# Recurrence of an RWKV-7 mixer: each head on its own rows and columns of TensorE, its two maps on top of each other

## The chip, the cores and the metric

The kernel runs on one core of a Trainium2 chip. The metric is the device time of one execution in microseconds. The kernel before took 2601.89 us (median of three runs, 2594.81 to 2606.95).

## The reference, cut to what matters

The program is one decoder block: a norm, one input projection, two causal token mixers side by side (an S5 state-space mixer and an RWKV-7 mixer), an output projection, and an MLP. The change lies in the recurrence of the RWKV-7 mixer, with 8 heads of 64 and 2048 tokens:

```python
def step(state, inp):
    r_t, d_t, k_t, v_t, kk_t, a_t = inp
    sa = jnp.einsum('bhvk,bhk->bhv', state, -kk_t)
    state = (state * d_t[:, :, None, :]
             + sa[..., None] * (kk_t * a_t)[:, :, None, :]
             + v_t[..., None] * k_t[:, :, None, :])
    return state, jnp.einsum('bhvk,bhk->bhv', state, r_t)
```

For each head a 64 by 64 state is multiplied by a decay, gets a rank-one correction from its own product with kk, and a rank-one update with v and k; the output is the state times r. All of it is float32.

## The kernel before, in words

**What runs when.** `hybrid_block` first does the S5 part and the input projection of the RWKV part (`rwkv_input`), which writes, by pair of heads, six rows of features to `f_d` in DRAM: k, v, b, a, q and bv, with the decays already worked in. `rwkv_phase` is the recurrence. Its first two blocks are prepared while `rwkv_input` still runs; the rest follows, and then the output projection and the MLP, which the change doesn't touch.

**The tiles of the recurrence.** The tokens are cut into 8 blocks of 256 (`TB`), a block into 4 chunks of 64 (`NCH`), and the 8 heads into 4 pairs (`NP`), so that a pair fills 128 partitions. One chunk is solved with matrices instead of token by token:

- `units(b, B, p)` (lines 806 to 832) takes one pair of one block. It loads b and a so that the two heads lie as blocks on the diagonal of a 128 by 128 tile (`ba`, zero elsewhere; `load_pair`, line 800, two DMAs), and a, q and k as they lie (`aq`, two DMAs). `ps_b` (line 817) multiplies b with a, q and an identity, 192 columns for each chunk; DVE masks the result and scales it into `bQ` (line 821), ACT scales the rest (line 822). `ps_a` (line 826) multiplies a with an identity and k for `aR`, 128 columns.
- `invert` (line 861) inverts 32 by 32 triangular matrices on DVE, 62 instructions a block (lines 876 and 877). Its input goes through DRAM: stores to `abd` (line 832), two loads into `M` (line 865); its result goes through `zd` (lines 880 and 882).
- `join` (line 884) couples the two halves of a chunk with matmuls of 32 by 32 (`ps_x`, line 898, first all of the one head's rows, then all of the other's; `ps_u`, line 905).
- `values(b, B, p)` (lines 834 to 859) loads k and v on the diagonal (`bk`, two DMAs), q as it lies (`qi`), and for each block q once more, transposed in its address pattern (`qS`, line 840). `ps_k` (line 853) multiplies k with q and an identity and makes `kT`; transposes (`ps_v`, line 851) make `vT`.
- `solve(B, u)` (line 908) takes one chunk: POOL builds `DT` from the inverse (four products, line 913, and two copies, line 917), `ps_pq` (line 920) multiplies it with `aR`, ACT copies the result into the diagonal blocks of `pq` in two copies (lines 923 and 924), then `ps_f` and `ps_h` (lines 928 and 930) multiply it with `bQ`. DVE adds q, the identity and `kT` (lines 934 to 936), which gives two maps: `gf` for the state and `hj` for the values.
- `chain(b, B, u, gf, hj)` (line 939) is the recurrence proper: for each pair `ps_s` accumulates `hj` with `vT` (line 949) and `gf` with the state `S` (line 951). The upper 64 rows of the result are the output, copied by ACT (line 958) and stored (line 963); the lower 64 rows times the decay (line 957, four DVE products a step, one for each half and head) are the next state, on the diagonal of `S`.

**What sets the order.** Between lines 1008 and 1073 the order of TensorE is written out by hand; the other engines are ordered by the scheduler. Step n does: the first half of the chain, the transposes left from the step before, the second half of the chain, `ps_pq` of chunk n + 2, `ps_b` of unit n + 13, `ps_k` of value n + 5, `ps_f` and `ps_h` of chunk n + 2, and `ps_a`. In the first step of a block `ps_x` and `ps_u` come in between. All loads and stores of this phase are issued by SP, in one queue, in order.

Of the kernel before, what the change touches and what calls it, by code (L numbers as in the profile page):

```python
# [15 lines left out]
P = 128  # L16
# [710 lines left out]
def consts_np():  # L727
# [10 lines left out]
    m4 = f((p // 32)[:, None] == (x // 32)[None, :])  # L738
    ist = f(s[:, None] == t64[None, :])
    parts = dict(ident=np.eye(P, dtype=np.float32), ones2=same, ma=lt, mk=ge, mb=np.concatenate([gt, ge], 1), off=off, m4=m4, ist=ist)  # L740
# [16 lines left out]
def rwkv_phase(K, f_dram, e_dram, n_dram, y_dram, ntok=2048):  # L757
# [7 lines left out]
    with ExitStack() as st:  # L765
# [6 lines left out]
        bas, aqs = [T([P, 2, NCH, P], f"ba{i}") for i in range(NB)], [T([P, 4, NCH, 64], f"aq{i}") for i in range(NB)]  # L772
        ist = c["ist"].rearrange("p (o x) -> p o x", o=1)
        for i in range(NB):
            g.memset(bas[i], 0.0)
            v.tensor_copy(aqs[i][:, 2], bc(ist, [P, NCH, 64]))
        S = None
# [3 lines left out]
        def begin(b):  # L781
# [3 lines left out]
                     abd=K.dram.tile([32, 4, 16, 32], F32, tag="abd", bufs=3, name="abd"),  # L785
# [12 lines left out]
        mask = lambda t, n: bc(t.rearrange("p (o x) -> p o x", o=1), [P, n, t.shape[1]])  # L798

        def load_pair(t, b, p, o):  # L800

            for h in range(2):
                hp = slice(h * 64, h * 64 + 64)
                nc.sync.dma_start(out=t[hp, :, :, hp].rearrange("p n c x -> p (n c) x"), in_=f_dram[p, hp, b, o:o + 2].rearrange("p n (c x) -> p (n c) x", x=64))

        def units(b, B, p):

            aR, bQ = B["aR"], B["bQ"]
            i = (b * NP + p) % NB
            ba, aq = bas[i], aqs[i]  # L810
            load_pair(ba, b, p, RW["b"])
            nc.sync.dma_start(out=aq[:, 0:2].rearrange("p n c x -> p n (c x)"), in_=f_dram[p, :, b, RW["a"]:RW["a"] + 2])
            nc.sync.dma_start(out=aq[:, 3].rearrange("p c x -> p (c x)"), in_=f_dram[p, :, b, RW["k"]])
            for uu in range(0, NCH, 2):
                psb = pp("ps_b")
                for u in range(2):
                    pe.matmul(psb[:, u * 192:(u + 1) * 192], ba[:, 0, uu + u], aq[:, 0:3, uu + u], start=True, stop=True)  # L817
# [7 lines left out]
            for u in range(NCH):  # L825
                pe.matmul(ps[:, u * P:(u + 1) * P], ba[:, 1, u], aq[:, 2:4, u], start=True, stop=True)
            v.tensor_tensor(out=aR[:, :, p, 0:64], in0=r4(ps)[:, :, 64:128], in1=mask(c["ma"], NCH), op=ALU.mult)
            act.copy(out=aR[:, :, p, 64:128], in_=r4(ps)[:, :, 0:64])
            if p == NP - 1:
                for hq in range(4):  # L830
                    q0 = (hq % 2) * 32
                    nc.sync.dma_start(out=B["abd"][:, hq], in_=bQ[hq * 32:(hq + 1) * 32, :, :, q0:q0 + 32].rearrange("s c p t -> s (c p) t"))

        def values(b, B, p):

            if p == 0:
                kv = kvs[b % 2]
                for n, shape in (("kT", [P, NCH, NP, P]), ("vT", [P, NCH, NP, P]), ("qS", [P, NP, TB])):
                    B[n] = kv.tile(shape, F32, tag=n, name=n)
                nc.sync.dma_start(out=B["qS"], in_=f_dram[:, :, b, RW["q"]].rearrange("t p n -> p t n"))  # L840
            kT, vT = B["kT"], B["vT"]
            i = (b * NP + p) % NB
            bk, qi = bks[i], qis[i]
            load_pair(bk, b, p, RW["k"])
            nc.sync.dma_start(out=qi[:, 0].rearrange("p c x -> p (c x)"), in_=f_dram[p, :, b, RW["q"]])
            for n in range(2):
                ps = pk("ps_" + "kv"[n])
                for u in range(NCH):
                    o = ps[:, u * P:(u + 1) * P]
                    if n:  # L850
                        pe.transpose(out=o, in_=bk[:, n, u], identity=K.ident)
                    else:
                        pe.matmul(o, bk[:, n, u], qi[:, :, u], start=True, stop=True)
                if n:
                    act.copy(out=vT[:, :, p], in_=r4(ps))
                else:
                    B["last"] = v.tensor_tensor(out=kT[:, :, p, 0:64], in0=r4(ps)[:, :, 0:64], in1=mask(c["mk"], NCH), op=ALU.mult)
                    act.copy(out=kT[:, :, p, 64:128], in_=r4(ps)[:, :, 64:128])
                    yield

        def invert(B, eng):

            M = un.tile([P, 32, 32], F32, tag="M", bufs=2, name="M")
            for par in range(2):
                nc.sync.dma_start(out=M[par * 64:par * 64 + 64], in_=B["abd"].rearrange("s q b t -> (q b) s t"))
# [42 lines left out]
        def solve(B, u):  # L908

            aR, kT, bQ, qS, dtc, cpl = B["aR"], B["kT"], B["bQ"], B["qS"], B["dtc"], B["cpl"]  # L910
            DT = bt.tile([P, NP, 4, 32], F32, tag="DT", name="DT")
            for p in range(NP):
                g.tensor_tensor(out=DT[:, p], in0=bc(dtc[:, u, p:p + 1, :], [P, 4, 32]),  # L913
                                in1=c["m4"].rearrange("p (a x) -> p a x", a=4), op=ALU.mult)
            for h in range(2):
                hs = slice(h * 64, h * 64 + 32)
                g.tensor_copy(DT[hs, :, 2 * h + 1], cpl[hs, u])
            ps = pb("ps_pq")
            for p in range(NP):
                pe.matmul(ps[:, p * P:(p + 1) * P], m2(DT, p), aR[:, u, p], start=True, stop=True)  # L920
            pq = pqs[u % 2]
# [66 lines left out]
        for t in pqs + Ss:  # L988
            g.memset(t, 0.0)
# [751 lines left out]
```

## Time and profile before

| what | value |
| --- | --- |
| median of three runs | 2601.89 us |
| the profiled execution's own time | 2604.97 us |
| its span, first to last instruction | 2603.2 us |
| mean granted clock of TensorE | 0.972 |
| PE busy | 2451.2 us, 94% of the span |
| recurrence after the input projection | about 655 to 991 us |
| ps_b, ps_a, ps_k, ps_pq, ps_f, ps_h | 256 instructions each |
| ps_s | 504 instructions |

A float32 matmul of the program is two pairs of a weight load (PEld) and a matmul (PE) in the trace, one pair for a transpose. In a line of a group the columns are the line, the engine, the operation, what is written and read, the shapes, the count, and then busy us, mean ns of one, and the idle time before with what ended it. For PE the two numbers such as 128*128 are rows and columns of the array that are used. Where a matmul's durations overlap, the time between the starts is its cost.

### The profile page before, as it was taken

To read this page: it belongs to the slowest core of one execution; us is meant where nothing else is said; L and a number is where in the kernel's file an instruction comes from. 1 tells how busy PE (TensorE), PEld (TensorE's weight loads), DVE (VectorE), ACT (ScalarE), POOL (GpSimd) and SP (SyncE) were. 2 spreads that over 40 slices of the span, in tenths; PEclk is the share of its full clock that TensorE was granted. 3 is DMA by queue.
4 is the path that set the end of the run, shared out by engine and by line. 5 is a ranking of instruction groups with operands and counts; after the bars stand their busy time and mean duration, and the time that the engine had idled before them with its cause. 6 is when DMAs were issued, how large, how long until landed. Compare 5 with 4: busy or idle time off the path is not lost.

```text
span 2603.2 us, 38292 instructions
## 1 busy us (share of the span) xinstructions
PE 2451.2 (94%) x13084; PEld 2030.0 (78%) x13084; DVE 1843.4 (71%) x3194; ACT 1302.0 (50%) x2551; POOL 858.4 (33%) x790
## 2 busy tenths in 40 slices
PE   7999979999898898999899999999989999999997
PEld 6887657786898887888688888888867877777775
DVE  7558797579677768666877678877766656665665
ACT  6355545465444446455476667666643323333333
POOL 1058798711222224221122320332212322332323
PEclk9999989999898998999999999999999999999998
DMA  9656737996776646443576566655495555544544
GB/s 287 206 166 177 221 115 231 251 259 176 181 153 156 145 101 199 145 149 115 178 241 216 198 208 220 242 205 198 166 355 195 175 173 164 171 158 154 186 150 166
DMA packets 540980, 491.50 MB, mean 189 GB/s; under 512 B 187281, under 2 KB 442769, under 8 KB 540785
## 3 DMA queue, kind: packets, MB, share of 16 engines
q1 hardware_dynamic: 539072, 483.54, 59.7%
q0 software_dynamic: 992, 3.67, 0.4%
q8 instruction: 104, 1.70, 0.3%
q10 hardware_dynamic: 720, 1.84, 0.2%
q14 instruction: 92, 0.75, 0.1%
HBM read 303.23 MB, written 180.49 MB: 186 GB/s over the span
## 4 chain that ended last, share of the span: by engine, by line
PE 63%; DVE 13%; DMA 10%; issue 5%; POOL 3%; ACT 3%; SPq 2%; POOLq 0%; ACTq 0%; DVEq 0%
PE ps_ua L1328 13%; PE ps_da L1328 9%; PE ps_ux L1328 7%; PE ps_dx L1328 4%; PE ps_ub L1328 3%; PE ps_db L1328 2%; DMA wraw<-in_w_down 2%; PE ps_o L435 2%; PE ps_o L433 2%; PE ps_o L434 2%; PE ps_z L433 1%; PE ps_z L434 1%; PE ps_z L435 1%; DMA hs<-hs_d 1%; PE ps_b L817 1%
## 5 line engine op out<-in xcount | busy, mean ns | idle before, releaser
L1620 POOL TENSOR_TENSOR acc<-acc,c 128x512 f32<-128x512 f32 x128 | 192.6, 1526 | 454.1 <-ACT c L1624 446.8
L1624 ACT COPY c<-ps_da 128x512 f32<-128x512 f32 x192 | 106.3, 588 | 262.6 <-PE ps_da L1328 261.1
L433 PE MATMUL ps_z<-xh,wh 128*128 128x512 f32 x448 | 183.8, 411 | 15.3 <-DVE zr L617 8.7
L435 PE MATMUL ps_z<-xh,wl 128*128 128x512 f32 x448 | 181.1, 405 | 0.0
L434 PE MATMUL ps_z<-xl,wh 128*128 128x512 f32 x448 | 180.3, 402 | 0.0
L1620 DVE TENSOR_TENSOR acc<-acc,ps_dx 128x512 f32<-128x512 f32 x128 | 87.5, 685 | 122.9 <-PE ps_dx L1328 120.7
L1425 DVE TENSOR_TENSOR wl<-wraw,wh 128x512 fp32r<-128x512 f32 x124 | 104.4, 843 | 28.1 <-ACT wh L1424 27.8
L374 ACT CAST hh<-hr 128x512 fp32r<-128x512 f32 x96 | 59.4, 620 | 117.7 <-PE ps_da L1328 90.4
L433 PEld LDWEIGHTS ps_z<-xh,wh 128*128 128x128 f32 x448 | 87.0, 194 | 40.0 <-DVE zr L617 10.5
L609 DVE TENSOR_TENSOR wl<-wr,wh 128x1024 fp32r<-128x1024 f32 x56 | 85.3, 1523 | 37.5 <-ACT wh L608 37.1
L913 POOL TENSOR_TENSOR DT<-dtc,cst 128x128 f32<-128x128 f32 x128 | 55.8, 467 | 158.2 <-PE ps_pq L920 105.9
L1291 POOL TENSOR_TENSOR ws<-wraw 128x512 f32<-128x512 f32 x28 | 41.2, 1471 | 200.6 <-DMA hs_d<-hh 72.6
L433 PE MATMUL ps_o<-woh,ys 128*128 128x512 f32 x256 | 103.0, 403 | 3.4 <-DVE xrow L1225 2.5
L1424 ACT CAST wh<-wraw 128x512 fp32r<-128x512 f32 x124 | 76.2, 617 | 52.9 <-PE ps_ua L1328 34.2
L434 PE MATMUL ps_o<-wol,ys 128*128 128x512 f32 x256 | 102.1, 399 | 0.0
L435 PEld LDWEIGHTS ps_z<-xh,wl 128*128 128x128 f32 x448 | 86.8, 194 | 19.1 <-issue 0.2
L434 PEld LDWEIGHTS ps_z<-xl,wh 128*128 128x128 f32 x448 | 87.0, 194 | 18.6 <-issue 0.9
L435 PE MATMUL ps_o<-woh,ys 128*128 128x512 f32 x256 | 100.7, 396 | 0.0
L1300 POOL TENSOR_TENSOR ws<-wraw,ws 128x512 f32<-128x512 f32 x28 | 41.7, 1489 | 176.0 <-DVE wl L1425 172.6
L1474 DVE TENSOR_TENSOR hh<-hs,hh 128x512 fp32r<-128x512 f32 x96 | 79.6, 829 | 14.2 <-ACT hh L1473 13.2
L1473 ACT CAST hh<-hs 128x512 fp32r<-128x512 f32 x96 | 59.7, 622 | 57.8 <-DVE hs L1490 21.3
L1425 DVE TENSOR_TENSOR wl<-ws,wh 128x512 fp32r<-128x512 f32 x93 | 66.7, 720 | 30.1 <-ACT wh L1424 25.9
(693 smaller groups left out, 8229.2 us busy)
## 6 DMA issues: line engine op xcount, KB each, us to landing
hs_d<-hh SPq DMA_DIRECT2D x256, 256.0 KB
hs<-hs_d SPq DMA_DIRECT2D x126, 512.0 KB
wraw<-in_w_up SPq DMA_DIRECT2D x62, 512.0 KB
wr<-in_w_in SPq DMA_DIRECT2D x56, 512.0 KB
hr<-hr_d SPq DMA_DIRECT2D x94, 256.0 KB
hr_d<-c SPq DMA_DIRECT2D x93, 256.0 KB
xrow<-in_x SPq DMA_DIRECT2D x32, 512.0 KB
wraw<-in_w_down SPq DMA_DIRECT2D x14, 1024.0 KB
```

Source lines behind the costliest of these rows:

```text
L374: nc.scalar.copy(out=hi, in_=raw)
L433: K.nc.tensor.matmul(out, lh, rh, start=i == 0, stop=False)
L434: K.nc.tensor.matmul(out, lh, rl, start=False, stop=False)
L435: K.nc.tensor.matmul(out, ll, rh, start=False, stop=i == n - 1)
L609: v.tensor_tensor(out=wl, in0=wr, in1=wh.bitcast(F32), op=ALU.subtract)
L1328: K.nc.tensor.matmul(ps, a[k], b[k], start=start and k + i == 0, stop=k == n - 1 and i == 2, skip_group_check=True)
L1424: act.copy(out=hi, in_=o)
L1425: v.tensor_tensor(out=lo, in0=o, in1=hi.bitcast(F32), op=ALU.subtract)
L1473: act.copy(out=hi, in_=o)
L1474: v.tensor_tensor(out=lo, in0=o, in1=hi.bitcast(F32), op=ALU.subtract)
L1620: add = lambda eng, o, s: eng.tensor_tensor(out=o, in0=o, in1=s, op=ALU.add)
L1624: act.copy(out=t, in_=ps)
```

## The change

The diagonal tiles go, and with them their zeros. Each head uses its own 64 rows and 64 columns of the array, and all operands are loaded as they lie in DRAM.

- `units` loads b, a and q in one DMA and k in another into one tile `rw`. `ps_b` and `ps_a` are two matmuls for each chunk, one for each head: rows `hs` of the operands, rows `hs` of the PSUM tile. Both heads write the same PSUM tile, on different partitions.
- `values` loads k and v in one DMA and q in another into `kv`. `ps_k` is done by head; its result goes to `KQ`, a tile with one map of 128 rows for each head: rows 0 to 63 what was `kT`, rows 64 to 127 what was added to the state map (q, copied by ACT, and an identity, written once at the start). The transposes now write 64 rows; they go to the upper half of `SV`. `qS` goes.
- `solve` makes `DT` with one POOL product (and two copies as before), `ps_pq` by head, one ACT copy into a dense `pq`. `ps_f` and `ps_h` become one product by head, with 64 rows and 128 columns of weights, so that the two maps come out on top of each other, each head in a PSUM tile of its own; DVE adds `KQ` with two products and gets `gh`.
- `chain` has one matmul for each head, with all 128 rows and 64 moving columns: the upper half of `SV` is the values, the lower half the state. One DVE product for each half (two a step) writes the next state into the lower half of the next chunk's `SV`.
- `abd` is laid out so that a load of `M` reads 4 KB in a piece where it read 128 bytes.

```diff
@@ rwkv_phase
-        bas, aqs = [T([P, 2, NCH, P], f"ba{i}") for i in range(NB)], [T([P, 4, NCH, 64], f"aq{i}") for i in range(NB)]
+        rws = [T([P, 5, NCH, 64], f"rw{i}") for i in range(NB)]
...
-                     abd=K.dram.tile([32, 4, 16, 32], F32, tag="abd", bufs=3, name="abd"),
+                     abd=K.dram.tile([4, 16, 32, 32], F32, tag="abd", bufs=3, name="abd"),
@@ units
-            load_pair(ba, b, p, RW["b"])
-            nc.sync.dma_start(out=aq[:, 0:2].rearrange("p n c x -> p n (c x)"), in_=f_dram[p, :, b, RW["a"]:RW["a"] + 2])
-            nc.sync.dma_start(out=aq[:, 3].rearrange("p c x -> p (c x)"), in_=f_dram[p, :, b, RW["k"]])
+            nc.sync.dma_start(out=rw[:, 0:3].rearrange("p n c x -> p n (c x)"), in_=f_dram[p, :, b, RW["b"]:RW["b"] + 3])
+            nc.sync.dma_start(out=rw[:, 4].rearrange("p c x -> p (c x)"), in_=f_dram[p, :, b, RW["k"]])
...
-                    pe.matmul(psb[:, u * 192:(u + 1) * 192], ba[:, 0, uu + u], aq[:, 0:3, uu + u], start=True, stop=True)
+                    for hs in heads:
+                        pe.matmul(psb[hs, u * 192:(u + 1) * 192], rw[hs, 0, uu + u], rw[hs, 1:4, uu + u], start=True, stop=True)
...
-                pe.matmul(ps[:, u * P:(u + 1) * P], ba[:, 1, u], aq[:, 2:4, u], start=True, stop=True)
+                for hs in heads:
+                    pe.matmul(ps[hs, u * P:(u + 1) * P], rw[hs, 1, u], rw[hs, 3:5, u], start=True, stop=True)
@@ values
+            nc.sync.dma_start(out=kv[:, 0:2].rearrange("p n c x -> p n (c x)"), in_=f_dram[p, :, b, RW["k"]:RW["k"] + 2])
+            nc.sync.dma_start(out=kv[:, 2].rearrange("p c x -> p (c x)"), in_=f_dram[p, :, b, RW["q"]])
+            ps = pk("ps_k")
+            for u in range(NCH):
+                for hs in heads:
+                    pe.matmul(ps[hs, u * P:(u + 1) * P], kv[hs, 0, u], kv[hs, 2:4, u], start=True, stop=True)
+            for h in range(2):
+                hp = slice(h * 64, h * 64 + 64)
+                B["last"] = v.tensor_tensor(out=KQ[0:64, :, h, p, 0:64], in0=r4(ps)[hp, :, 0:64], in1=mask(c["mk"][hp], NCH, 64), op=ALU.mult)
+                act.copy(out=KQ[0:64, :, h, p, 64:128], in_=r4(ps)[hp, :, 64:128])
+                act.copy(out=KQ[64:128, :, h, p, 0:64], in_=kv[hp, 2])
+            yield
+            ps = pk("ps_v")
+            for u in range(NCH):
+                pe.transpose(out=ps[0:64, u * P:(u + 1) * P], in_=kv[:, 1, u], identity=K.ident)
+            act.copy(out=SV[0:64, :, p], in_=r4(ps)[0:64])
@@ invert
-                nc.sync.dma_start(out=M[par * 64:par * 64 + 64], in_=B["abd"].rearrange("s q b t -> (q b) s t"))
+                nc.sync.dma_start(out=M[par * 64:par * 64 + 64], in_=B["abd"].rearrange("q b s t -> (q b) s t"))
@@ solve
-            for p in range(NP):
-                g.tensor_tensor(out=DT[:, p], in0=bc(dtc[:, u, p:p + 1, :], [P, 4, 32]),
-                                in1=c["m4"].rearrange("p (a x) -> p a x", a=4), op=ALU.mult)
+            g.tensor_tensor(out=DT, in0=bc(dtc[:, u].rearrange("p a (o t) -> p a o t", o=1), [P, NP, 2, 32]),
+                            in1=bc(c["m2"].rearrange("p (o a t) -> p o a t", o=1, a=2), [P, NP, 2, 32]), op=ALU.mult)
...
-                pe.matmul(ps[:, p * P:(p + 1) * P], m2(DT, p), aR[:, u, p], start=True, stop=True)
-            pq = pqs[u % 2]
-            psr = ps.rearrange("p (a q x) -> p a q x", a=NP, q=2)
-            act.copy(out=pq[0:64, :, :, 0:64], in_=psr[0:64])
-            act.copy(out=pq[64:128, :, :, 64:128], in_=psr[64:128])
+                for hs in heads:
+                    pe.matmul(ps[hs, p * P:(p + 1) * P], m2(DT, p)[hs], aR[hs, u, p], start=True, stop=True)
+            pq = bt.tile([P, NP, P], F32, tag="pq", name="pq")
+            act.copy(out=f2(pq), in_=ps)
             yield
-            psf, psh = pb("ps_f"), pb("ps_h")
-            for p in range(NP):
-                pe.matmul(psf[:, p * P:(p + 1) * P], pq[:, p, 1], bQ[:, u, p, 64:192], start=True, stop=True)
-            for p in range(NP):
-                pe.matmul(psh[:, p * P:(p + 1) * P], pq[:, p, 0], bQ[:, u, p, 64:192], start=True, stop=True)
...
+            ph = [pb("ps_h") for _ in range(2)]
+            for p in range(NP):
+                for h in range(2):
+                    hs = slice(h * 64, h * 64 + 64)
+                    pe.matmul(ph[h][:, p * P:(p + 1) * P], pq[hs, p], bQ[hs, u, p, 64:192], start=True, stop=True)
+            gh = bt.tile([P, 2, NP, P], F32, tag="gh", bufs=3, name="gh")
+            for h in range(2):
+                B["last"] = v.tensor_tensor(out=f2(gh[:, h]), in0=ph[h], in1=f2(B["KQ"][:, u, h]), op=ALU.add)
@@ chain
-                    pe.matmul(pss[:, o], hj[:, p], vT[:, u, p], start=True, stop=S is None)
-                    if S is not None:
-                        pe.matmul(pss[:, o], gf[:, p].rearrange("p q x -> p (q x)"), S[:, p], start=False, stop=True)
+                    for h in range(2):
+                        o = (2 * (p - p0) + h) * 64
+                        pe.matmul(pss[:, o:o + 64], gh[:, h, p], SV[:, u, p, h * 64:h * 64 + 64], start=True, stop=True)
...
-                for h in range(2):
-                    hs = slice(h * 64, h * 64 + 64)
-                    e = em[64:128, p0:p0 + 2, h, b * NCH + u:b * NCH + u + 1]
-                    v.tensor_tensor(out=new[hs, p0:p0 + 2, hs], in0=pv[64:128, :, h], in1=bc(e, [64, 2, 64]), op=ALU.mult)
+                if n + 1 < nb * NCH:
+                    to = SVs[(n + 1) // NCH % 2][64:128, (n + 1) % NCH, p0:p0 + 2].rearrange("p a (h x) -> p (a h) x", h=2)
+                    v.tensor_tensor(out=to, in0=pss[64:128, 0:2 * P].rearrange("p (a x) -> p a x", a=4),
+                                    in1=bc(em[64:128, 2 * p0:2 * p0 + 4, n:n + 1], [64, 4, 64]), op=ALU.mult)
@@ set-up
-            g.memset(bks[i], 0.0)
-            v.tensor_copy(qis[i][:, 1], bc(ist, [P, NCH, 64]))
+        for t in KQs:
+            for h in range(2):
+                for u in range(NCH):
+                    v.tensor_copy(t[64:128, u, h, :, 64:128], bc(ist[64:128], [64, NP, 64]))
+        g.memset(SVs[0][64:128, 0], 0.0)
```

More of the change, by code (lines that the diff above doesn't have):

```diff
@@ L737, in consts_np @@
     off = f((h[:, None] == (x // 64)[None, :]) & ((s < 32)[:, None]) & ((x % 64 >= 32)[None, :]))
-    m4 = f((p // 32)[:, None] == (x // 32)[None, :])
+    m2 = f((s // 32)[:, None] == (t64 // 32)[None, :])
     ist = f(s[:, None] == t64[None, :])
-    parts = dict(ident=np.eye(P, dtype=np.float32), ones2=same, ma=lt, mk=ge, mb=np.concatenate([gt, ge], 1), off=off, m4=m4, ist=ist)
+    parts = dict(ident=np.eye(P, dtype=np.float32), ones2=same, ma=lt, mk=ge, mb=np.concatenate([gt, ge], 1), off=off, m2=m2, ist=ist)
     offs, o = {}, 0
@@ L797, in rwkv_phase @@
         r4 = lambda t: t.rearrange("p (c x) -> p c x", c=NCH)
-        mask = lambda t, n: bc(t.rearrange("p (o x) -> p o x", o=1), [P, n, t.shape[1]])
-        def load_pair(t, b, p, o):
-            for h in range(2):
-                hp = slice(h * 64, h * 64 + 64)
-                nc.sync.dma_start(out=t[hp, :, :, hp].rearrange("p n c x -> p (n c) x"), in_=f_dram[p, hp, b, o:o + 2].rearrange("p n (c x) -> p (n c) x", x=64))
+        mask = lambda t, n, rows=P: bc(t.rearrange("p (o x) -> p o x", o=1), [rows, n, t.shape[1]])
+        heads = [slice(h * 64, h * 64 + 64) for h in range(2)]
         def units(b, B, p):
             aR, bQ = B["aR"], B["bQ"]
-            i = (b * NP + p) % NB
-            ba, aq = bas[i], aqs[i]
-            load_pair(ba, b, p, RW["b"])
-            nc.sync.dma_start(out=aq[:, 0:2].rearrange("p n c x -> p n (c x)"), in_=f_dram[p, :, b, RW["a"]:RW["a"] + 2])
-            nc.sync.dma_start(out=aq[:, 3].rearrange("p c x -> p (c x)"), in_=f_dram[p, :, b, RW["k"]])
+            rw = rws[(b * NP + p) % NB]
+            nc.sync.dma_start(out=rw[:, 0:3].rearrange("p n c x -> p n (c x)"), in_=f_dram[p, :, b, RW["b"]:RW["b"] + 3])
+            nc.sync.dma_start(out=rw[:, 4].rearrange("p c x -> p (c x)"), in_=f_dram[p, :, b, RW["k"]])
             for uu in range(0, NCH, 2):
@@ L831, in units @@
                     q0 = (hq % 2) * 32
-                    nc.sync.dma_start(out=B["abd"][:, hq], in_=bQ[hq * 32:(hq + 1) * 32, :, :, q0:q0 + 32].rearrange("s c p t -> s (c p) t"))
+                    nc.sync.dma_start(out=B["abd"][hq].rearrange("b s t -> s b t"), in_=bQ[hq * 32:(hq + 1) * 32, :, :, q0:q0 + 32].rearrange("s c p t -> s (c p) t"))
         def values(b, B, p):
[L836 to L859, printed above, removed]
+            KQ, SV = KQs[b % 2], SVs[b % 2]
@@ L934, in solve @@
-            v.tensor_tensor(out=gf[:, :, 0], in0=pf[:, :, 0], in1=qS[:, :, u * 64:(u + 1) * 64], op=ALU.add)
-            v.tensor_tensor(out=gf[:, :, 1], in0=pf[:, :, 1], in1=bc(ist, [P, NP, 64]), op=ALU.add)
-            B["last"] = v.tensor_tensor(out=f2(hj), in0=psh, in1=f2(kT[:, u]), op=ALU.add)
-            yield gf, hj
-        def chain(b, B, u, gf, hj):
-            nonlocal S
-            vT = B["vT"]
+                for h in range(2):
+                    hs = slice(h * 64, h * 64 + 64)
+                    pe.matmul(ph[h][:, p * P:(p + 1) * P], pq[hs, p], bQ[hs, u, p, 64:192], start=True, stop=True)
```

36 lines of the change are left out of this document (15 added, 21 removed).

## The prediction, made before the changed kernel was run

> **What bounds the kernel now.** I read the page first, then busy time by stretch over the recurrence, the timeline of TensorE inside one step, the chain of waits, the queue of SP, and last the groups of DVE and ACT there. The page:
>
> ```profile
> span 2603.2 us, 38292 instructions
> PE 2451.2 (94%) x13084; PEld 2030.0 (78%) x13084; DVE 1843.4 (71%) x3194; ACT 1302.0 (50%) x2551; POOL 858.4 (33%) x790
> ```
>
> PE carries the kernel, but an average says nothing of the stage that changes. That stage runs from about 655 to 991 us. I cut it where a block of four steps begins (a step is 64 tokens, a block 256); columns are length, then busy PE, PEld, DVE, ACT, POOL, the granted clock, and the DMA share:
>
> ```profile
> 655.60:706.30 50.70, 44.98 (x402) 42.54 (x402) 31.20 (x102) 21.53 (x55) 15.04 (x36) 0.86 0.82 181
> 706.30:744.90 38.60, 37.32 (x403) 36.34 (x402) 33.08 (x118) 18.36 (x47) 10.14 (x27) 1.00 0.71 158
> 744.90:793.50 48.60, 42.41 (x403) 41.38 (x402) 35.44 (x123) 20.63 (x51) 10.08 (x28) 0.86 0.68 154
> 793.50:837.40 43.90, 39.80 (x403) 39.06 (x403) 33.89 (x118) 19.79 (x49) 10.05 (x27) 0.92 0.68 156
> 837.40:879.10 41.70, 38.63 (x403) 37.89 (x402) 33.37 (x118) 19.61 (x48) 10.09 (x27) 0.96 0.71 162
> 879.10:915.40 36.30, 32.75 (x369) 31.91 (x368) 29.30 (x102) 16.84 (x39) 9.36 (x24) 1.00 0.54 116
> 915.40:946.70 31.30, 28.56 (x338) 27.57 (x337) 24.08 (x75) 12.92 (x27) 8.58 (x22) 1.00 0.46 109
> 946.70:991.00 44.30, 39.00 (x402) 37.04 (x403) 27.18 (x65) 24.97 (x49) 11.42 (x26) 0.96 0.55 164
> ```
>
> The four blocks in the middle do the same work (403 instructions of PE) in 38.6, 48.6, 43.9 and 41.7 us. The first is the clean one: PE at full clock, 1.3 us idle. The others lose 3 to 10 us to idleness and to the low clock behind it. DVE needs 33 to 35 us, so it is the next limit, close under PE. One step on PE:
>
> ```profile
> 810.98 0.49 PE L949 MATMUL ps_s<-vT,hj 128*128 128x128 f32 x2
> ...
> 811.97 0.60 PE L851 MATMUL ps_v<-cst,bk 128*128 128x128 f32 x4
> ...
> 813.30 1.06 PE L920 MATMUL ps_pq<-aR,DT 128*128 128x128 f32 x8
> 814.20 1.47 PE L817 MATMUL ps_b<-aq,ba 128*128 128x192 f32 x8
> 815.50 1.05 PE L853 MATMUL ps_k<-qi,bk 128*128 128x128 f32 x8
> 816.39 1.06 PE L928 MATMUL ps_f<-bQ,pq 128*128 128x128 f32 x8
> 817.28 1.06 PE L930 MATMUL ps_h<-bQ,pq 128*128 128x128 f32 x8
> 818.18 1.06 PE L826 MATMUL ps_a<-aq,ba 128*128 128x128 f32 x8
> 819.07 0.39 PE L949 MATMUL ps_s<-vT,hj 128*128 128x128 f32 x2
> ```
>
> The step takes 8.09 us with no hole. By differences of starts, a group of eight instructions takes 0.89 us at 128 columns (0.111 each; each f32 matmul of the program is two of them) and 1.30 us at 192. ps_s, in pieces from 810.98 to 813.30 less the transposes' 0.44, has 16 instructions at 0.111, 1.78 us.
>
> The lost time is seen in the chain of waits, and in SP's queue before it:
>
> ```profile
> 822.15 5.56 DMA lo<-zd
> 827.76 2.05 PE ps_k L853 x8
> 829.80 1.71 PE ps_f L928 x8
> ```
>
> ```profile
> 815.30 2.71 SPq L865 DMA_DIRECT2D M<-abd  x2
> 818.05 1.50 SPq L963 DMA_DIRECT2D y_d<-Y  x1
> 820.84 1.27 SPq L804 DMA_DIRECT2D bk<-f_d  x2
> ```
>
> PE stands still until 827.76 and then does eight instructions in 2.05 and 1.71 us instead of 0.89. The chain names lo, but ps_k reads bk, issued just ahead of lo on the same queue; bk waited behind the inverter's M loads, which SP needs 2.71 us to issue.
>
> **The change part by part.** (1) The products per head. ps_b, ps_a, ps_k and ps_pq become two matmuls of 64 rows and 64 columns each, on opposite corners of the array, with as many moving columns as before. One after the other they would cost twice; side by side, the same. Does this array run two such matmuls together? The trace has one place where neighbours use different rows: ps_x does 32 instructions on rows 0 to 31 and then 32 on rows 64 to 95. Counting what is in flight at one instant (a window of a nanosecond; PE first, PEld second):
>
> ```profile
> 837.70:837.70 0.00, 0.00 (x6) 0.00 (x4) 0.00 (x0) 1.00 0.00 0
> 838.38:838.38 0.00, 0.00 (x9) 0.00 (x6) 0.00 (x0) 1.00 1.12 256
> 838.70:838.70 0.00, 0.00 (x6) 0.00 (x3) 0.00 (x0) 1.00 0.00 0
> ```
>
> In the middle of either run six matmuls and three or four loads are in flight; where the row groups change, nine and six. So matmuls and weight loads of different row groups do overlap, in f32, some three deep, and a stream that alternates heads every two instructions asks for less than that. I take full overlap: cost 0 against before. The other end is none: 1.30 + 0.89 + 0.89 + 0.89 = 3.97 us more in each of the 32 steps.
>
> (2) The maps. ps_f and ps_h (16 instructions, 1.78 us) become 16 on halves of the rows, in pairs with a PSUM bank each: 0.89 us by the same overlap. Their weights are 64 rows of 128 columns. A load of 128 columns after another:
>
> ```profile
> 846.50 0.30 PEld L949 LDWEIGHTS ps_s<-vT,hj 128*128 128x128 f32 x2
> ```
>
> Two loads of 0.192 us end 0.30 after the first began: 0.108 apart. If loads of the two halves took turns, ps_h would stay at 16 x 0.108 = 1.73 us; the six loads in flight above speak for overlap. I take 0.89, a saving of 0.89. The Trainium skill, TensorE: Matmul & The Clock Gate, section "LDWEIGHTS (loading the stationary operand)", says a load's time goes with its columns alone, so that half the rows save nothing; 128/1.2 ns is 107 ns, which the trace's 0.108 bears out, and if such loads also took turns the saving would be 0.05.
>
> (3) The state. ps_s keeps 16 instructions with 64 columns instead of 128, but still 128 columns of weights each. At 0.108 a load they cannot come faster than 16 x 0.108 = 1.73 us: saving 0.05, at the very best 0.89.
>
> (4) Leaving and entering small tiles. ps_b straight behind ps_x's 32 by 32 tiles, and ps_b in a step without them:
>
> ```profile
> 839.47 1.50 PE ps_b L817 x8
> ...
> 849.88 1.30 PE ps_b L817 x8
> ```
>
> That is 0.20 us for one change of tile shape. A step gets up to four (full to 64x64 at ps_pq, to 64x128 at ps_h, back at ps_a, full at ps_s): 0 to 0.8 us; I take 0.4, since a change may be milder between halves. The transposes for V keep all rows and only write fewer columns: 0.
>
> PE per step: -0.89 - 0.05 + 0.4, about -0.5, 2 us a block.
>
> (5) Loads. Each units and each values pass issued two loads of 64 x 8 pieces of 256 bytes beside its plain ones; now it has two loads with rows of 1 to 3 KB, and the 512 KB for qS are gone. M was 2 x 2048 pieces of 128 bytes; now 64 rows of 4 KB, so SP's 2.71 us should fall to about twice the 0.64 that one of L804's takes (1.27 for two). So SP gives out the values' load some 3 us or more sooner, into rings that carry less. The load landed 5.6 us behind its issue; I expect the stall and the low clock behind it to go nearly entirely. What is late next is PE itself.
>
> (6) The other engines, by groups between 700 and 980 us:
>
> ```profile
> L957 DVE TENSOR_TENSOR S<-ps_s,em 64x128 f32<-64x128 f32 x116 | 34.1, 294 | 12.4 <-PE ps_s L951 10.0
> L936 DVE TENSOR_TENSOR hj<-ps_h,kT 128x512 f32<-128x512 f32 x29 | 19.9, 686 | 3.5 <-PE ps_h L930 2.3
> L924 ACT COPY pq<-ps_pq 64x512 f32<-64x512 f32 x30 | 17.4, 581 | 0.7
> L934 DVE TENSOR_TENSOR gf<-ps_f,qS 128x256 f32<-128x256 f32 x29 | 12.2, 421 | 11.0 <-PE ps_f L928 10.9
> L857 DVE TENSOR_TENSOR kT<-ps_k,cst 128x256 f32<-128x256 f32 x27 | 11.3, 418 | 9.9 <-PE ps_k L853 9.7
> ```
>
> DVE: four state products of 0.294 become two of 64x256 (priced as L934's 0.421), -0.34; L934, L935 and L936, 0.42 + 0.42 + 0.69, become two of L936's size, -0.15; the mask product L857 becomes two on 64 rows, +0.42. Nothing in sum, so DVE's 33 us a block stay and are the floor. ACT: the two pq copies (0.58 each) become one, and three short ones come (two for q into KQ, and KQ's copy out of PSUM in two halves), at most 0.58 each; with 20 busy of 40 us this hides, and the one on the way from ps_pq to ps_h is 0.58 shorter. POOL's four DT products become one and its zero fills go: hidden, off the path. At the start DVE gets 16 small identity copies for KQ, at most 0.4 each by L934: hidden in the 19.5 us that it idles from 655.6 to 706.3, and 2 us late where they are not.
>
> The sum, against the profiled 2604.97 us (span 2603.2 and 1.8 around it; the median of the runs is 3 us lower). Clean block: 37.3 - 2 of PE and 1.3 idle is 36.6; I allow 37.5. Four of them against 38.6 + 48.6 + 43.9 + 41.7 = 172.8: 150, -23. The stretches from 879.1, 915.4 and 946.7: -2 of PE each, and some 1 of idleness from the shorter copy: -9. The first, 655.6 to 706.3, at clock 0.86: -3. The eight units of the first two blocks run earlier, between full-size products, and pay two changes of shape each, 16 x 0.2 = +3; the identity copies +2. In all -30: 2575 us.
>
> **The rivals.** (A) Slower: the two heads do not run together where they write one PSUM bank. In ps_x the two runs wrote different banks; ps_b, ps_a, ps_k and ps_pq write theirs into one, on different partitions, and no row here shows that. Price: 32 x 3.97 = 127 more, ps_f's 28 less, 13 for changes of shape, and of the stalls 25 saved: 2605 + 87 = 2692. Since a full miss is 127 and the forecast 30, it decides from the point where a quarter of the pairs fail to overlap. The Trainium skill, TensorEngine Tiling (Array Packing), section "Restrictions and Gotchas", states that different row tiles cannot access the same PSUM bank simultaneously; by that rule this is the outcome, though it does not say whether column halves on separate partitions count, and no run here shows it. Chance 0.17.
>
> (B) No change: the map products do not get shorter because their loads take turns (1.73 us, as above). 32 x 0.84 = 27 of the 30 are gone: 2602. The same comes out if every change of shape costs 0.2 and part of the stalls stays. For it: DVE at 33 of 38 us leaves little slack, so each late operand shows. Against it: loads in flight six deep. Chance 0.17.
>
> (C) Faster still: ps_s goes by its 64 moving columns, 32 x 0.84 = 27 more: 2548. Against it, the 0.108 of a load; DVE's floor would catch it too. Chance 0.06.
>
> **How the numbers follow.** Forecast 0.60, of which its own bounds (changes of shape 0 to 0.8 us a step, 13 us each way; half of the 25 us of stalls) make 2555 to 2595. No change of this kernel under about 0.5% (13 us) can be told from nothing. Faster: 0.56 of the forecast and all of C, 0.62. Same: most of B and the forecast's upper edge, 0.17. Slower: A and a little of B, 0.21. For eight in ten the range reaches from 2550 to 2620; A and most of C are left out.
>
> **What would show it.** PE in a step: ps_b still 1.3 us and ps_a, ps_k, ps_pq 0.89 for twice the instructions, with starts in pairs; ps_h alone 0.89; ps_s about 1.75. Blocks of 36 to 38 us, full clock, no hole ahead of ps_k; SP issuing M in about a microsecond; the DMA share under 0.6; DVE's busy time a block unchanged. The prediction is wrong if ps_b takes 2.6 us (A), if ps_h stays at 1.7 (B), or if holes of 3 us remain ahead of ps_k.

## The result, and the profile after

The changed kernel takes 2681.62 us (median of four runs, 2677.86 to 2689.64) against 2599.59 us before: a ratio of 1.0318, 95% interval 1.0298 to 1.0337. It is slower by about 80 us; the forecast was 2575, with a range of 2550 to 2620. The page of the profile after:

```profile
span 2680.8 us, 40056 instructions
PE 2493.5 (93%) x14116; PEld 2035.4 (76%) x14116; DVE 1853.0 (69%) x3144; ACT 1320.5 (49%) x2615; POOL 818.5 (31%) x687
```

PE is busy for 42 us more than before, with nearly the same share of the span (93% for 94%). The recurrence, cut where ps_x starts, as it was cut for before (length, then busy PE, PEld, DVE, ACT, POOL, the granted clock, DMA share, GB/s):

```profile
658.40:719.70 61.30, 49.77 (x587) 42.40 (x588) 38.75 (x129) 26.87 (x72) 5.15 (x14) 0.81 0.49 136
719.70:771.80 52.10, 44.53 (x532) 38.70 (x530) 34.90 (x110) 21.79 (x57) 5.87 (x15) 0.79 0.41 110
771.80:827.60 55.80, 45.41 (x531) 39.96 (x529) 35.05 (x110) 21.80 (x57) 5.86 (x15) 0.78 0.39 103
827.60:880.10 52.50, 44.05 (x532) 38.25 (x531) 34.98 (x110) 21.86 (x57) 5.88 (x15) 0.83 0.41 109
880.10:935.50 55.40, 46.22 (x532) 40.35 (x531) 35.02 (x110) 21.86 (x57) 5.88 (x15) 0.78 0.39 103
...
1016.20:1073.00 56.80, 41.05 (x451) 37.52 (x448) 33.85 (x58) 28.54 (x56) 19.71 (x21) 0.79 0.53 167
```

The stretches come in the same order as before's, one for one. Before, the four whole blocks took 38.6 to 48.6 us; now they take 52 to 56, the stretch ahead of them 61.3 for 50.7, the one at the end 56.8 for 44.3. From the first cut to the last the recurrence takes 414.6 us, where it took 335.4, so the whole loss lies in it. DVE's busy time in a block is 35 us (33 to 35 before), and the DMA share fell from 0.7 to 0.4, both about as predicted. But PE idles 7.6 to 10.4 us in each block, and runs at a granted clock of 0.78 to 0.83 around that.

One block by its four steps says where. First the kernel after: the step ahead of ps_x, the step with ps_x, and the two that follow. Then the kernel before, whose lines begin with the step with ps_x and end with the step ahead of the next ps_x:

```profile
861.80:878.20 16.40, 10.85 (x103) 9.37 (x102) 15.09 (x53) 4.85 (x13) 0.72 (x1) 0.80 0.28 80
878.20:897.90 19.70, 16.35 (x230) 14.16 (x229) 11.17 (x34) 7.33 (x18) 1.89 (x6) 0.73 0.38 96
897.90:908.00 10.10, 9.93 (x103) 9.10 (x105) 4.54 (x12) 3.86 (x11) 1.98 (x6) 0.83 0.25 41
908.00:917.10 9.10, 7.90 (x100) 6.79 (x100) 4.13 (x12) 5.13 (x14) 1.29 (x3) 1.00 0.76 223
```

```profile
836.40:848.80 12.40, 12.40 (x198) 12.08 (x197) 11.20 (x38) 6.75 (x16) 2.96 (x8) 1.00 0.59 162
848.80:857.20 8.40, 8.40 (x72) 8.25 (x71) 8.00 (x32) 4.20 (x11) 2.40 (x6) 1.00 0.61 130
857.20:865.20 8.00, 8.00 (x71) 8.00 (x70) 4.21 (x13) 3.43 (x9) 2.98 (x9) 1.00 1.02 171
865.20:878.10 12.90, 9.83 (x71) 9.56 (x70) 9.97 (x36) 5.34 (x14) 1.75 (x4) 0.87 0.69 178
```

Read the DVE column. DVE's work in a block is the same, but in the changed kernel 15.09 us of it (53 instructions) stand in the step of 16.4 us, 11.17 in the next, and 4 us in each of the last two, where DVE has nothing to do for half of the time. Of those 53 instructions, 41 are the inverter's products (counted in the trace); the four lines hold 41, 18, 0 and 3 of them. Before, the lines quoted hold 24, 16, 2 and 19, the first 40 the end of one inverse, the other 21 the beginning of the next. From its first product to its last, an inverse in the middle blocks takes 24 us in the changed kernel and 34 to 36 in the kernel before. The step with 15 us of DVE work lasts 16.4 us, though TensorE is busy in it for 10.85. What PE waits for in it:

```profile
861.76 1.09 PE L911 MATMUL ps_pq<-aR,DT 64*64 64x128 f32 x16
862.68 1.47 PE L811 MATMUL ps_b<-rw 64*64 64x192 f32 x16
865.78 1.09 PE L840 MATMUL ps_k<-kv 64*64 64x128 f32 x16 [1.64 <-ACT SV L850]
868.30 2.08 PE L920 MATMUL ps_h<-bQ,pq 64*128 64x128 f32 x16 [1.42 <-ACT pq L913]
870.30 1.74 PE L821 MATMUL ps_a<-rw 64*64 64x128 f32 x16
...
875.57 1.06 PE L849 MATMUL ps_v<-cst,kv 128*64 128x128 f32 x4 [2.50 <-ACT KQ L844]
```

The brackets are idle time and what ended it: ACT copies, but these stand behind others for which ACT waited for DVE. The products of DVE in that time:

```profile
866.88 0.43 DVE L940 TENSOR_TENSOR SV<-ps_s,em 64x256 f32<-64x256 f32 x1
867.34 0.28 DVE L868 TENSOR_TENSOR Z<-Z,prod 128x115 f32<-128x115 f32 x1
867.65 0.28 DVE L867 TENSOR_TENSOR prod<-Z,M 128x110 f32<-128x110 f32 x1
...
869.89 0.30 DVE L868 TENSOR_TENSOR Z<-Z,prod 128x133 f32<-128x133 f32 x1
870.22 0.35 DVE L815 SCALAR_TENSOR_TENSOR bQ<-ps_b,n,cst 128x128 f32<-128x128 f32 x1
```

Between the second state product (L940) and the first scaling of ps_b's result (L815) nine of the inverter's instructions (L867, L868) take 2.9 us, in DVE's fixed order, while ps_b has been there since about 864. That state product itself comes 5 us after its ps_s, which ended at 861.8, with products of the inverter in between; ACT's copy of the output waits for it until 867.40, the copy of pq follows on ACT at 867.67, and ps_h can start at 868.30. The step with ps_x has a second queue in it, ACT's:

```profile
838.12 0.37 ACT L844 COPY KQ<-ps_k 64x256 f32<-64x256 f32 x1 [0.49 <-DVE KQ L843]
842.64 0.83 ACT L845 COPY KQ<-kv 64x256 f32<-64x256 f32 x2 [4.15 <-DMA kv<-f_d]
843.49 0.37 ACT L823 COPY aR<-ps_a 128x256 f32<-128x256 f32 x1
843.76 1.17 ACT L897 COPY cpl<-ps_u 32x512 f32<-32x512 f32 x2
```

The two new copies of q into KQ (L845) wait 4.15 us for the load of q, and the copies of ps_a's and ps_u's results, which ps_pq needs (the second by way of DT), wait behind them. Over 700 to 1050 us the view of waits has for this:

```profile
ACT KQ L845 <- DMA kv<-f_d: 44.5, 19, 5.9
```

(44.5 us in total, 19 times, the longest 5.9.) Two causes are thus in sight: the place of the inverter in DVE's order (theory 1), and the q copies in ACT's queue (theory 2). The rival, theory 3: the halved tiles, or the longer chain into KQ (DVE, ACT, DVE, ACT where it was DVE, ACT), are slow by themselves.

### The profile page after: what moved, and what is told of

Its sections match the earlier page's. It is cut to its first block, busy times and chain, and to the rows that moved or that the text cites. A ratio compares the mean times of both kernels' runs of the same rounds, so it can differ in the third digit from the quotient of the medians.

```text
span 2680.8 us, 40056 instructions
## 1 busy us (share of the span) xinstructions
PE 2493.5 (93%) x14116; PEld 2035.4 (76%) x14116; DVE 1853.0 (69%) x3144; ACT 1320.5 (49%) x2615; POOL 818.5 (31%) x687
## 4 chain that ended last, share of the span: by engine, by line
PE 49%; DVE 6%; DMA 5%; ACT 2%; issue 1%; POOL 1%; SPq 0%; POOLq 0%; ACTq 0%; DVEq 0%
PE ps_ua L1312 13%; PE ps_da L1312 9%; PE ps_ux L1312 7%; PE ps_dx L1312 4%; PE ps_ub L1312 3%; DMA wraw<-in_w_down 3%; PE ps_db L1312 2%; PE ps_o L433 2%; PE ps_o L434 2%; PE ps_o L435 2%; DMA hs<-hs_d 1%; DVE acc L1604 1%; PE ps_s L936 1%; POOL acc L1604 1%; DVE wraw L1299 1%
## 5 line engine op out<-in xcount | busy, mean ns | idle before, releaser
L1284 POOL TENSOR_TENSOR ws<-wraw,ws 128x512 f32<-128x512 f32 x28 | 41.7, 1488 | 176.8 <-DVE wl L1409 167.5
L903 POOL TENSOR_TENSOR DT<-dtc,cst 128x256 f32<-128x256 f32 x32 | 24.0, 751 | 222.4 <-PE ps_pq L911 173.9
L815 DVE SCALAR_TENSOR_TENSOR bQ<-ps_b,n,cst 128x128 f32<-128x128 f32 x128 | 43.0, 348 | 64.4 <-PE ps_b L811 32.3
```

## The experiments

**The inverse left out, in both kernels** (called a_inv0 and b_inv0; a stands for the changed kernel, b for the kernel before). 60 of the 62 products of an inverse are not done.

```diff
-            for s in range(31):
+            for s in range(1):
```

> The changed kernel with 60 of the 62 DVE products of each 32 by 32 inverse left out (so the inverse is not computed). Theory 1, order on DVE: the inverter's products stand in runs of two to nine in front of the products that PE and ACT wait for, in two of the four steps of a block. Without them these two steps (16.4 and 19.7 us) fall to the 8.5 us of the other two plus 4 for the 32 by 32 tiles: a block of 52 to 56 us falls to about 38, five blocks, 2682 - 75 = about 2605, granted clock in the blocks near 1.0. Theory 2, ACT's queue: the q copies wait for loads just as before, 2650 or more. Theory 3, the halved tiles themselves run slowly or cold: the clock in the blocks stays at 0.8 and the time above 2660.

> The kernel before with the same 60 products of each inverse left out: the control. Theory 1: its order spreads the inverter's products thinly, so they cost it little, the stalls at ps_k being of the loads: blocks of 40 to 43 instead of 43.2 us, 2580 to 2600. If DVE bounds both kernels alike, it gains as much as the changed one, some 75 us.

Measured: a_inv0 2616.83 us, 65 less than the changed kernel, ratio to before 1.0045 (1.0026 to 1.0064). b_inv0 2567.87, ratio 0.9872 (0.9846 to 0.9897): 36 less than before. A block of b_inv0, and one of a_inv0:

```profile
739.10:775.80 36.70, 36.70 (x402) 36.26 (x401) 20.09 (x57) 19.59 (x49) 9.73 (x27) 1.00 0.80 185
```

```profile
842.70:885.50 42.80, 37.70 (x531) 32.96 (x529) 19.38 (x49) 21.78 (x56) 5.09 (x12) 0.92 0.50 135
```

With the inverse gone, TensorE never idles in this block of the kernel before, at a DMA share of 0.8, and the holes ahead of ps_k are gone with it: they were not a matter of the loads alone, as the prediction had it. (The view of waits of b_inv0 has no load ahead of ps_k, and its middle blocks all take 36.7 to 36.9 us.) In a_inv0 the middle blocks take 41.7 to 47.4 us: the steps without ps_x take 7.4 to 10, but the step with ps_x still takes 18 to 22, where b_inv0 has 12.5. So theory 1's 2605 was missed by 12 us, and b_inv0 gained more than theory 1 allowed it. Without the inverse the changed kernel is still 49 us slower than the kernel before without it: the inverter is a part of the loss, and not all of it.

**q by DMA** (a_qdma): theory 2 alone.

```diff
-                act.copy(out=KQ[64:128, :, h, p, 0:64], in_=kv[hp, 2])
+                nc.sync.dma_start(out=KQ[64:128, :, h, p, 0:64], in_=f_dram[p, hp, b, RW["q"]].rearrange("p (c x) -> p c x", x=64))
```

> The changed kernel with q brought into the lower rows of KQ by two DMAs in place of ACT's two copies. Theory 2, ACT's queue: the 44 us in which ACT stands in front of these copies waiting for a load go, and what is behind them (the copies of cpl and of pq) comes earlier: about 2640. Theory 1: only the part of them that ends in PE's wait for DT in the step after ps_u goes, 2 us a block: 2665 to 2680.

**The inverter spread** (a_spread): theory 1 alone. Its pairs of products are tied singly behind other DVE products, 9, 9, 9 and 4 pairs in four steps.

```diff
+                if inv is not None:
+                    k = min(QUOTA[u], left)
...
+                    for j in range(k):
+                        with tc.issue_after(marks[j * len(marks) // k]):
+                            next(inv)
```

> The changed kernel with all its work, but the inverter's products tied one pair at a time behind the other DVE products of four steps (9, 9, 9 and 4 pairs) in place of all in two steps. Theory 1: no run of them is longer than about 1 us, blocks fall from 54 to about 40 us: 2600 to 2620. Theory 2 or 3: 2660 or more.

**Both** (a_spread_qdma).

> The changed kernel with both suspects taken away at once: the inverter's pairs of products are tied one by one behind other DVE products over four steps (9, 9, 9, 4), and q reaches KQ by two DMAs in place of two ACT copies. Theory 1 (the order of the inverter on DVE) and theory 2 (q copies that hold ACT's queue) together: each alone left the step with ps_x at 17 to 18.5 us; if nothing else delays it, it falls to about 12.5 to 13.5, as in the kernel before, the blocks are 37 to 40 us, and the time is 2656 less 4 blocks of 4 us and some for the first stretch, 2620 to 2640. If the chain KQ DVE, ACT, DVE, ACT by itself delays it (third theory), the step stays at 17 or more and the time within 10 us of 2656.

Measured: a_qdma 2676.10 us (ratio to before 1.0279, 1.0252 to 1.0306), a_spread 2655.73 (1.0206, 1.0185 to 1.0226), both 2644.13 (1.0139, 1.0116 to 1.0162). So the q copies are worth some 5 us, within what theory 1 expected and far from theory 2's 2640; the inverter spread is worth 26, which lies between what theory 1 (2600 to 2620) and the others (2660 or more) expected. Two steps of a_spread, the one ahead of ps_x and the one with it:

```profile
841.90:849.80 7.90, 7.86 (x103) 6.99 (x102) 6.89 (x25) 4.06 (x11) 0.77 (x3) 1.00 0.59 136
849.80:867.00 17.20, 14.94 (x229) 12.81 (x228) 12.62 (x38) 8.38 (x21) 1.97 (x4) 0.80 0.44 132
```

The step ahead of ps_x falls from 16.4 to 7.9 us: theory 1 is right there. The step with ps_x stays at 17 to 18.6 us in the middle blocks of all three, so the two theories, as stated, don't cover it, and 2644 lies 4 us over the range that they gave; the step is what the third theory expected, though the time is 2 us under its 10 us around 2656. But the trace of both together shows another thing. ps_x of the block from 846 us starts 2.05 us late, because DVE's transpose of the inverse waits 2.37 us for the inverse to come back by DMA. Over 700 to 1050 us the view of waits has for this:

```profile
PE ps_x L896 <- DVE up L886: 15.6, 5, 5.1
```

The changed kernel and a_qdma have no such wait, a_spread has 10.4 us of it: spreading the inverse has made it. DVE's product for aR and its state products stand behind that transpose, up to 848.6, and ACT behind them: it idles 6.1 us until 847.4, and the copies of ps_x's result come at 850.0 and 850.6, with ps_x done at 849.0. That is an order too, only not one of the two that were removed.

**The orders of DVE and ACT by hand** (a_hand; the same for the kernel before, b_hand). Both engines, like TensorE, now follow the order in which the program writes the steps, with the inverter's pairs written singly between the other products. (In the cut below, tick() writes the next pair of the inverter, if the step's share isn't used up.)

```diff
-        with tc.manual_schedule(engines={mybir.EngineType.PE}):
+        QUOTA = (9, 9, 9, 4)
+        with tc.manual_schedule(engines={mybir.EngineType.PE, mybir.EngineType.DVE, mybir.EngineType.Activation}):
...
                 B["last"] = v.tensor_tensor(out=f2(gh[:, h]), in0=ph[h], in1=f2(B["KQ"][:, u, h]), op=ALU.add)
+                tick()
...
-                        for _ in invert(Bs[m // NP], v):
-                            pass
+                        iv.update(it=invert(Bs[m // NP], v, True), left=31)
+                        next(iv["it"])
```

> The changed kernel, with the order of DVE and ACT, too, as the program writes it through the recurrence, and the inverter's pairs written singly between the products of the steps (9, 9, 9, 4 a block). If the orders on DVE and ACT alone lost the time (theories 1 and 2 as one: the arithmetic on TensorE is sound, the queues around it are not), blocks fall to 36 to 40 us, the last stretch to 41 us, and the time to 2585 to 2620. If the smaller tiles themselves or the KQ chain lose it, blocks stay at 43 or more, and the time over 2640.

> The kernel before with the same orders written out by hand and the same quotas of the inverter. It says what the order alone is worth: before's blocks of 38.6, 48.6, 43.9 and 41.7 fall to 37 to 38 us if its stalls were the inverter's place on DVE (as its run with the inverse left out had 36.8), and the time to 2570 to 2585. If the late load of bk was the cause, as the prediction had it, blocks stay above 42 and the time at 2590 or more. The change by itself is then read from the pair a_hand and b_hand.

> a_hand with the q copies of ACT replaced by two DMAs into KQ. If ACT's queue still stands behind the q load (theory 2) with its order written out, this is 5 us or more a block faster than a_hand; if the order alone was it, the two agree within 10 us.

Measured: a_hand 2610.03 us, ratio to before 1.0015 (1.0001 to 1.0029). No operation was changed or left out, and some 72 of the 80 us are back. Two blocks of a_hand, the step with ps_x, and another step on TensorE:

```profile
746.10:784.90 38.80, 36.46 (x530) 32.09 (x531) 33.22 (x110) 21.94 (x56) 5.78 (x15) 1.00 0.54 144
...
823.80:862.60 38.80, 36.45 (x529) 32.06 (x529) 33.21 (x110) 21.95 (x56) 6.07 (x16) 1.00 0.56 145
...
822.30:835.80 13.50, 12.19 (x230) 10.78 (x229) 11.85 (x36) 7.40 (x18) 1.81 (x4) 1.00 0.46 138
```

```profile
853.27 1.09 PE L930 MATMUL ps_pq<-aR,DT 64*64 64x128 f32 x16
854.19 1.47 PE L823 MATMUL ps_b<-rw 64*64 64x192 f32 x16
855.49 1.04 PE L854 MATMUL ps_k<-kv 64*64 64x128 f32 x16
856.46 1.16 PE L939 MATMUL ps_h<-bQ,pq 64*128 64x128 f32 x16
857.56 1.09 PE L834 MATMUL ps_a<-rw 64*64 64x128 f32 x16
858.58 1.10 PE L956 MATMUL ps_s<-SV,gh 128*128 128x64 f32 x8
859.67 0.63 PE L864 MATMUL ps_v<-cst,kv 128*64 128x128 f32 x4
860.13 1.00 PE L956 MATMUL ps_s<-SV,gh 128*128 128x64 f32 x8
861.06 1.09 PE L930 MATMUL ps_pq<-aR,DT 64*64 64x128 f32 x16
```

DVE does the same work, 33 us, in a block of 38.8, TensorE has the full clock in these two blocks and 0.96 in the two other middle ones, and the step with ps_x takes 13.5 to 14.6 us (12.4 before) with the chain into KQ and with the q copies as the change wrote them. Theory 3 falls but for a microsecond or two in that step, and the q copies do no harm where they stand in their turn: a_hand_qdma, at 2619.85 (1.0052, 1.0033 to 1.0072), is 10 us slower than a_hand.

b_hand did not gain: 2625.08 (1.0070, 1.0046 to 1.0094), slower than before, with blocks of 44 us, where 37 to 38 was expected if the inverter's place was what stalled the kernel before. Its ps_x waits for the inverse's way back (15.8 us over 700 to 1050 us). An order by hand is no gain as such; for that kernel the scheduler's own was better.

**Each queue alone, and a fairer partner** (a_hand_dve, a_hand_act: only the one engine's name in the set; b_hand_q: the kernel before by hand with shares 11, 11, 9, 0).

> a_hand, with only DVE's order as the program writes it (and the inverter's pairs singly between the steps' products); ACT's order is left to the planner again. If DVE's queue carries the loss, blocks stay at 38.8 to 40 us and the time within 12 us of a_hand (2600 to 2622). If ACT's queue (q copies and up copies that stand ahead of what is due) carries it, blocks go back to 45 or more, and the time to 2640 or more.

> a_hand, with only ACT's order as the program writes it; DVE's order is left to the planner. The mirror of the run with DVE's alone: if DVE's queue carries the loss, blocks stay at 48 us or more, and the time over 2650; if ACT's does, blocks fall under 42 us, and the time to 2600 to 2625. Should both runs stop half way (blocks of 43 to 45, 2630 to 2650), the loss is in the two orders together, neither queue alone.

> The kernel before with its orders written out, and the inverter's shares 11, 11, 9, 0 in place of 9, 9, 9, 4, so that the inverse is written out and read back one step earlier. In b_hand the product of up waited for that way back (17 us of waits at ps_x between 700 and 1050 us; the step ahead of ps_x took 19 us), so it was no fair partner of a_hand. If that was its loss, the step falls to 8 to 13 us, blocks to 37 to 39 us, and the time to 2575 to 2595, and what the change does to TensorE alone is then about nothing or a loss beside a_hand's 2610. If it stays at 2615 or more, the loss lies in something else of the order.

Measured: a_hand_dve 2624.45 (1.0068, 1.0042 to 1.0094), a_hand_act 2684.48 (1.0298, 1.0269 to 1.0326), b_hand_q 2622.02 (1.0064, 1.0040 to 1.0087). A middle block of a_hand_dve, and one of a_hand_act:

```profile
795.50:836.10 40.60, 37.66 (x529) 32.74 (x529) 33.55 (x109) 21.84 (x56) 5.75 (x16) 0.96 0.53 144
```

```profile
831.70:885.20 53.50, 43.38 (x532) 37.72 (x530) 34.37 (x110) 22.98 (x59) 5.84 (x15) 0.81 0.42 110
```

DVE's order carries most of the loss: mended alone it gives 57 of the 80 us (blocks of 40.6 to 41.4 us, a little over what was expected); ACT's, alone, nothing; ACT's after DVE's is mended, 14 more. One rival is left: SP's queue was not written by hand, but the scheduler gave it another order along with DVE's, so loads came at other times. The traces speak against it. In the changed kernel, over 700 to 1050 us, PE waits for no load of the recurrence; ACT's q copies wait 44.5 us for theirs, and in a_hand_dve they still wait 37.4 us, with 57 us of time gained.

In b_hand_q the wait of ps_x is mostly gone, as expected (4.5 us are left; blocks still 44 to 45), and now TensorE waits for what a load brings:

```profile
PE ps_k L867 <- DMA lo<-zd: 16.2, 4, 4.6
```

That is the hole that the prediction described, four times up to 4.6 us in this window, of 700 to 950 us; in the changed kernel with its orders by hand, same window, ps_k waits for no load. As in the prediction, the name lo is the last load of the queue and ps_k's own is another; which one held it was not tried.

**The last stretch** (a_hand_tail, a_hand_tail2, a_best). In a_hand the recurrence ended at 996 us, 9 us after before's, with work of the next phase ahead of the last steps' products. a_hand_tail ties that work on DVE and ACT behind the third step from the end; a_hand_tail2 ties it on DVE, ACT and TensorE behind the last map; a_best also moves the last inverse forward (shares 11, 16, 4, 0).

```diff
+            with tc.issue_after(K.tail[0]), tc.issue_after(K.tail[1]), tc.issue_after(K.tail[2]):
                 opened = out_proj(K, keep,
...
```

> a_hand with the work of the phase behind the recurrence (splits of its weights, its first sums) queued on DVE and ACT behind the first state of the third step from the end. In a_hand such work stands ahead of the last steps' products, with TensorE idle for 3.6, 3.5 and 6.1 us between 962 and 993 us of its span; the last state product is at 996.0 where the kernel before has it at 987.3. If that order is the whole of the lost tail, the last ps_s comes at 982 to 986 and the time falls by 5 to 12 us under a_hand, to 2598 to 2605, just under the kernel before. If the next phase lives on that early work, the end of the recurrence moves and the time does not: within 4 us of a_hand.

> a_hand with all instructions of the phase behind the recurrence queued on DVE, ACT and TensorE behind the last gh, pq and ps_h product of the recurrence. In the run that tied them on DVE and ACT alone, three steps from the end, a transpose of the next phase (ps_gt) stood ahead of ps_h on TensorE and waited for its load (3.6 us of idleness), and gh stood 8 us behind weight splits. If the mixed tail is what keeps the version with the orders by hand from beating both kernels, the last ps_s comes at 980 to 986 in place of 996 to 998, and the time at 2590 to 2600, ratio 0.995 to 0.999. If that early work is needed where it stands, the time stays within 4 us of 2607, or rises.

> The changed kernel with orders by hand and the tail tied, and the last inverse's shares 11, 16, 4, 0 in place of 9, 9, 9, 4. In the run without this the last inverse ended at 927.6 us of the span, its way out and back put the product of up at 939.2, and ps_x of the last block at 940.7, 41.1 us behind the one before it, where the kernel before has 31.3. If that lateness alone holds the last block, ps_x comes at 930 to 934, the last ps_s at 974 to 978, and the time at 2592 to 2600, ratio about 0.996: a version faster than both. If another chain holds it, or the saving is taken up by the phase behind, the ratio stays within 0.998 to 1.001.

Measured: 2606.47 us (ratio 1.0009, 0.9993 to 1.0025), 2605.73 (0.9994, 0.9981 to 1.0008) and 2602.68 (1.0001, 0.9986 to 1.0017). The first did not move the end of the recurrence (998 us), since TensorE still stood at a transpose of the next phase:

```profile
972.57 0.48 PE L1149 MATMUL ps_gt<-cst,grow 128*128 128x128 f32 x1 [3.67 <-DMA grow<-g_d]
972.98 2.08 PE L939 MATMUL ps_h<-bQ,pq 64*128 64x128 f32 x16
```

With that tied too, the last ps_s came at 983.1 us, as expected, and in a_best at 980.5, against 987.3 before. The time of the whole kernel did not follow: all three are the kernel before within 0.3%. a_best missed its ps_x (937.5 us, where 930 to 934 was expected), its last ps_s (974 to 978) and with them the 2592 to 2600 us that hung on these. No version tried that does all the work is faster than the kernel before.

## Why the prediction was wrong, point by point

- **(1) The products per head: right.** In a_hand's step the 16 instructions of ps_pq take 0.92 us, those of ps_b 1.30, of ps_k 0.97 (starts to next starts); one after the other would be 1.78 and 2.60. Rival A named this as the place where the kernel would lose, at 2692 us. The time came out near that by luck, not by its mechanism: both heads write one PSUM tile and run side by side. The Trainium skill, TensorEngine Tiling (Array Packing), section "Restrictions and Gotchas", says that different row tiles cannot access the same PSUM bank at the same time; here that doesn't hold, for these tiles lie on opposite corners and differ in columns, too. For column tiles the Trainium skill, PSUM — Partial Sum Buffer, section "PSUM bank collisions raise a hardware error", allows one bank on disjoint partitions, and the 0.92 us agrees with that.
- **(2) The maps: right in the mechanism.** ps_h takes 1.10 us with its change of shape where ps_f and ps_h took 1.78. Rival B's first way, loads that take turns, falls. Its time, 2602, is what came out with the orders by hand and the tail tied, and for it the prediction had a second way: changes of shape, and DVE with little slack.
- **(3) The state: right, and a little worse.** Each half of ps_s takes 0.93 to 1.09 us for eight instructions, 1.78 in all before and 2.02 now: half the moving columns, with weights of 128 columns still, gained nothing. Rival C falls. The Trainium skill, TensorE: Matmul & The Clock Gate, section "LDWEIGHTS (loading the stationary operand)", says that a load's time goes with its columns; the trace agrees, with 0.116 us each in the faster half where it was 0.111.
- **(4) Changes of shape: mis-sized.** A step of a_hand without a hole takes 7.79 us against 8.09 before: -0.3, where the sum had -0.5. By block, TensorE is busy 36.45 us at full clock against b_inv0's 36.70 without a hole, so the change saves TensorE about a quarter of a microsecond a block, and not 2.
- **(5) The loads: right in what the change does, wrong in what follows.** M is issued in less than before's 2.71 us, though not in the 1.27 or so that was forecast (the queue's row after, its line of SP):

```profile
852.78 1.87 SPq L856 DMA_DIRECT2D M<-abd  x2
```

  The DMA share fell to 0.4, and no load stands ahead of ps_k any more. Two steps failed here. The first is the cause of the lost time before, put down to the late load alone: b_inv0 does the same loads and has no wait of ps_k for one, with blocks of under 37 us, and the view of waits before has no more than 11.5 us of ps_k waiting for a load in the whole recurrence (660 to 990 us). The second is "What is late next is PE itself." What was late next was DVE. With it went the 23 us that four blocks were to save; they lost 43 instead (215.8 us for 172.8).
- **(6) The other engines: this failed with it.** "Nothing in sum, so DVE's 33 us a block stay and are the floor" is right as a sum and says nothing of the steps. 33 of 38 us is a floor only if the work lies evenly; with 15.1 us of it in one step of four, that step is about as long as DVE is busy. And "with 20 busy of 40 us this hides" left out that ACT works in order: a copy that waits 4 us for its load holds those behind it, though a_qdma shows that this alone costs some 5 us. All of the 0.21 for a slower kernel was given to A and a little of B; no rival had the orders of DVE and ACT in it. The prediction took the orders of DVE and ACT as they were, though the scheduler makes them anew for each kernel.
- **The clock** went with it, and more than doubled the price. In the block from 880.1 us, 9.2 us of idleness come with a granted clock of 0.78, at which the same 530 instructions keep PE busy 46.22 us; in a_hand it is 36.45 at 1.00. Of the 16.6 us between the two blocks 9.8 are longer busy time, and 6.8 more idleness.

What stays open: why the scheduler put 41 of the 62 products into one step of the changed kernel. That this order, together with ACT's, costs the time is shown by a_hand and a_hand_dve; which edit of the change brought it about was not tried.

## What to carry to other kernels

Where a scheduler orders an engine, its order belongs to the kernel that it was made for: when a change alters the operations around it, ask of each engine that is nearly full how its work lies in each step, not in the sum over a block. To tell a slow operation from a bad order, write the order out by hand and change nothing else; if the time comes back, the operations were sound. And when one suspect is moved, look in the new trace for the wait that the move has made: spreading the inverse made ps_x wait for its way back, 15.6 us in all.

## What the runs showed of the hardware that was not expected

Two float32 matmuls on opposite corners of the array run side by side, even into one PSUM tile: sixteen in 0.92 us where eight of full size took 0.89. What the merged maps gain on TensorE (1.10 us for 1.78 in a step) is mostly paid back where the shape of the tiles changes: ps_k, ps_a and ps_h take 0.08 to 0.21 us more than the 0.89 of eight full-size instructions, and a step is 0.3 us shorter. And idleness came with a granted clock of 0.73 to 0.83 around it: in the pair of blocks above, 6.8 us more of idle time went with 16.6 us of length.
